# Encoder trunk: memory keys of layer 1 first, residual pieces turned by DMA, first loads in another order

## The chip, the core and the metric

The kernel runs on one core of a Trainium2 chip. The metric is the device time of one execution in microseconds; the number given for a kernel is the median of its timed runs. A profiled execution has a time of its own and a span (from the first to the last instruction in the trace).

## What is computed

Two encoder layers over 256 tokens of width 2048, in float32, each followed by a SwiGLU block. A layer norms x, makes one combined projection for a token mixer and for four memory heads, joins their outputs, projects back and adds. Layer 0 mixes by spatial gating, layer 1 by grouped-query attention with rotary tables. In both, the memory heads attend to 256 memory tokens, whose keys and values come from `mem` alone:

```python
def memory_attention(q_mem, mem, g_mem, w_kv, g_mq, g_mk):
    kv = rms_norm(mem, g_mem) @ w_kv
    k, v = jnp.split(kv, 2, axis=-1)
    k = rms_norm(k.reshape(B, -1, MEM_HEADS, HEAD_DIM), g_mk)
    q = rms_norm(q_mem.reshape(B, S, MEM_HEADS, HEAD_DIM), g_mq)
    s = jnp.einsum('bshd,bmhd->bhsm', q, k).astype(jnp.float32) * (HEAD_DIM ** -0.5)
    p = jax.nn.softmax(s, axis=-1).astype(v.dtype)
    return jnp.einsum('bhsm,bmhd->bshd', p, v)

for l in range(DEPTH):
    h = rms_norm(x, g_mix[l])
    # layer 0: z = h @ w_in_a, gating; layer 1: z = h @ w_in_b, attention; q_mem is the last part of z
    x = x + jnp.concatenate([tok_out, mem_out], axis=-1) @ w_out[l]
    x = x + swiglu(rms_norm(x, g_ffn[l]), w_gate_up[l], w_down[l])
```

## The kernel before

Every float32 operand is split into two parts, a rounded `hi` (ScalarE) and the rest `lo` (VectorE), and each product is made of three matmuls (`matmul3`, L181 to L183). The left operand are the *parts* of an activation, 16 chunks of 128 features by 256 tokens; the right one are weights, loaded raw by SP into buffers of four chunks (`raw`, four of them), cast to `whi` (L265) and subtracted to `wlo` (L266), three buffers of four chunks each.

A `Linear` makes 512 output columns from 16 chunks: 96 matmuls of 512 columns into two of four PSUM banks (`acc`). After every two chunks (12 matmuls) it calls `tick()`, which advances a clock and runs what other code has put off with `later(delay, fn)`; this, and the order of the program, gives the order of the work around the matmuls. The compiler's scheduler then orders each engine's queue by readiness and by that order.

Parts are made in four ways. At the start, x already turned is loaded in eight pieces (`load_turned`) and split by `gained_pair` (`first_piece`, L237 and L238); the squares for its norm come from x itself, loaded by `load_x` and squared by `first_squares` (L207). The memory tokens, also turned already, are loaded on GpSimd's queue and split by the same `gained_pair` (`Memory.prep`: eight loads, each split three ticks after). Between layers, a piece of the new x (512 columns of 128 tokens) is turned either by PE (`norm_piece`: four transposes at L187, into PSUM) or by a DMA transpose (`turned`: a copy that parts the 16-bit halves, L194, the DMA on ScalarE's queue, L195, and a copy that joins them, L200), and then split by `gained` (L225, L226). `residual_turns` takes the DMA for the columns j = 0, 1, which are complete while the last pair of the down projection still runs, and PE for j = 2, 3. Attention heads are turned by PE (`heads_T`, `turn`).

Attention is a chain on later ticks: `head_norm` (squares L449, factors L455, scaling L459, which reads the linear's banks), `queries`, `scores` (exponentials L513, scaling L518), `turn` (transposes L528), `weigh`; four delays say at which ticks.

All parts and attention tiles of a layer's mixer come from one room of 36 tiles (`big`, `MIX_TILES`); a tile that finds none free waits. The room of layer 1 lies on the memory of layer 0's feed-forward room.

Layer 0 runs: warm-up matmuls on an identity, the first linear in pieces of one and two chunks as they land, three linears of v, q_mem, memory keys, memory values, three of u, the output projection. Layer 1 runs:

```python
load_tables(1)
m.prep(20, 2)
acc = linear(hT, w, TOK)                      # own keys
own["v"] = scaled(linear(hT, w, TOK + MEMW), norm.r)
for c in range(3):                            # three groups of queries
    acc = linear(hT, w, c * NB)
    attend(head_norm(acc, norm.r, ghead["q"], True), (5, 6, 10, 13), ...)
m.attend(linear(hT, w, TOK + 2 * MEMW), norm.r, cat)
m.keys()
m.values()
```

The functions that the change touches, with the line numbers of the profile:

Of the kernel before, what the change touches and what calls it, by code (L numbers as in the profile page):

```python
# [17 lines left out]
P = 128  # L18
# [37 lines left out]
def encoder(ctx: ExitStack, tc: tile.TileContext, x, x_t, mem, mem_t, columns, w_in_a, g_v_a, spatial_t, w_in_b,  # L56
# [14 lines left out]
    def nm(s):  # L71
        uid[0] += 1
        return f"{s}_{uid[0]}"
# [195 lines left out]
    class Linear:  # L269
# [3 lines left out]
            self.parts, self.w, self.n0, self.left, self.first, self.raw = parts, w, n0, nk, True, {}  # L273
            self.acc = [psa.tile([P, NB], F32, tag="acc", name=nm("acc")) for _ in range(NT)]

        def fetch(self, k0, n):
            raw = wp.tile([P, KC4, NB], F32, tag="raw", name=nm("raw"), bufs=RAW_TILES)
            src = self.w[k0 * P:(k0 + n) * P, self.n0:self.n0 + NB]
            nc.sync.dma_start(raw[:, :n], src.rearrange("(c p) n -> p c n", p=P))
            self.raw[k0] = raw  # L280

        def run(self, units):
            for k0, n in units:
                if k0 not in self.raw:
                    self.fetch(k0, n)
                raw = self.raw.pop(k0)
                parts = halves(raw[:, :n], n, KC2)
                for s in range(0, n, KC2):
                    m = min(KC2, n - s)
                    self.left -= m  # L290
                    for t in range(NT):
                        for c in range(m):
                            matmul3(self.acc[t], self.parts.get(k0 + s + c, t), parts[s + c],
                                    self.first and c == 0, self.left == 0 and c == m - 1)
                    self.first = False
                    tick()
            return self.acc
# [270 lines left out]
    class Memory:  # L568
# [5 lines left out]
        def prep(self, delay, apart):  # L574
            def load(i):
                m = big(shape=[P, 2, S])
                nc.gpsimd.dma_start(m, mem_t[:, 2 * i:2 * i + 2])
                later(3, lambda: gained_pair(m, i, gslice("mem", self.l), self.parts, big))
                if self.l == 0:
                    j, t = i // 2, i % 2  # L580
                    rows = big()
                    nc.gpsimd.dma_start(rows, mem[0, t * P:(t + 1) * P, j * NB:(j + 1) * NB])
                    later(3, lambda: squares(rows, j, t))

            def squares(rows, j, t):
                self.norm.add(rows, t, j)
                if (j, t) == (3, NT - 1):
                    self.norm.finish(self.r)

            for i in range(8):  # L590
                later(delay + apart * i, lambda i=i: load(i))

        def keys(self):
            acc = linear(self.parts, w_mem_kv[self.l], 0)
# [6 lines left out]
        def values(self):  # L601
            self.V = scaled(linear(self.parts, w_mem_kv[self.l], NB), self.r)

        def attend(self, acc, r, parts):
            attend(head_norm(acc, r, ghead[f"mq{self.l}"]), (4, 13, 17, 19), lambda: self.kT, lambda: self.V, lambda h: h,
                   TOK // P, parts)

    def add_residual(acc, j, norm, g, parts, dma):

# [12 lines left out]
            later(1 + t, lambda t=t: turn(t))  # L622

    def residual_turns(j, norm, g, parts):
        add_residual(None, j, norm, g, parts, j < 2)


    hT = Parts()
# [1 line left out]
    for l in range(DEPTH):  # L630
# [4 lines left out]
        if l == 0:  # L635
# [51 lines left out]

            turned_x = {}
            lin = Linear(hT, w, TOK)
            load_turned(0, nc.scalar)  # L690
            nc.scalar.dma_start(cols, columns)
            nc.scalar.activation(junk[:, :8], mhalf, AF.Square)
            warm_up(9)
            lin.fetch(0, 1)
            lin.fetch(1, 1)
            load_turned(1)
            lin.fetch(2, 2)
            first_piece(0)
            lin.run([(0, 1)])
            load_turned(2)  # L700
            load_turned(3)
            lin.run([(1, 1)])
            first_piece(1)
            lin.run([(2, 2)])
            for i in range(2, 8):
                first_piece(i)
                if i % 2 == 0 and i < 6:
                    load_turned(i + 2)
                    load_turned(i + 3)
                lin.run([(2 * i, KC2)])  # L710
            for t in range(NT):
                for j in range(4):
                    load_x(t, j)
            load_tables(0)
            for j in range(4):
                first_squares(j)
            norm.finish()
            acc = lin.acc
            m.prep(1, 2)
            for i in range(3):  # L720
                later(10 + i, lambda i=i: load_spatial(i))
            for c in range(3):
                if c:
                    acc = linear(hT, w, TOK + c * NB)
                for t in range(NT):
                    v[t][c] = big()
                    nc.scalar.activation(v[t][c], acc[t], AF.Gelu, scale=norm.r[t])
                    square_sum(v[t][c], ssv[t][:, 2 * c:2 * c + 2])
            for t in range(NT):
                gate_rms(t)  # L730
                for c in range(3):
                    later(3 + 3 * t + c, lambda t=t, c=c: gate(t, c))
# [10 lines left out]
        else:  # L743
            w = w_in_b[0]
            own = {}
            load_tables(1)
            m.prep(20, 2)
            acc = linear(hT, w, TOK)
            kn = head_norm(acc, norm.r, ghead["k"], True)

# [5 lines left out]
            for c in range(3):  # L756
                acc = linear(hT, w, c * NB)
                attend(head_norm(acc, norm.r, ghead["q"], True), (5, 6, 10, 13), lambda: own["k"], lambda: own["v"],
                       lambda h, c=c: (4 * c + h) // 3, 4 * c, cat)
            m.attend(linear(hT, w, TOK + 2 * MEMW), norm.r, cat)  # L760
            m.keys()
            m.values()

        hF = Parts()
# [130 lines left out]
```

## Time and profile before

| | |
|---|---|
| timed runs | 2009.22 us median of three, 2007.90 to 2009.52 |
| profiled execution | 2011.89 us, span 2010.0 us |
| mean granted TensorE clock | 0.998 |
| busy: PE, VectorE, ScalarE, GpSimd | 99%, 79%, 60%, 3% |
| first matmul of the first linear | 6.78 us after the span's start |
| first matmul of layer 1 | 1007.5 us |
| first matmul of layer 1's memory keys | 1156.95 us |

In the profile, PE is TensorE's matmuls, PEld its weight loads, DVE VectorE, ACT ScalarE, POOL GpSimd, SP the engine that issues most DMAs. A row of the timeline begins with start and duration in us; in brackets stands how long the engine was idle before and what released it. Matmuls overlap: one of 512 columns is shown with 0.39 us, while a new one starts every 0.23. PEclk is the granted share of TensorE's clock. A group of instructions gives count, busy us and mean ns of one, then idle time before them and its releasers.

### The profile page before, as it was taken

Reading aid. Unit: us, or ns where it says so; the run is one execution under the profiler, and the core shown is the slowest. Engines: PE = TensorE matmul, PEld = TensorE weight load, DVE = VectorE, ACT = ScalarE, POOL = GpSimd, SP = SyncE. Lnnn points to the kernel's source line nnn. Section 1 sums busy time; section 2 is a strip of 40 time slices with the busy share of each in tenths; the row PEclk is TensorE's granted clock in tenths of the full one; section 3 lists DMA queues with packets and bytes.
Section 4 is the critical chain, followed back from the end, with each engine's and each line's share of the span. In section 5 each row is a group of like instructions: output and inputs, shape, how many; then the busy total and the mean of one; then the engine's idle time right before and its main releaser. Section 6 shows DMA issues by size and latency. Waiting matters only on the chain.

```text
span 2010.0 us, 23977 instructions
## 1 busy us (share of the span) xinstructions
PE 1994.3 (99%) x8996; PEld 1652.5 (82%) x8996; DVE 1587.4 (79%) x1686; ACT 1204.0 (60%) x1450; POOL 60.3 (3%) x88
## 2 busy tenths in 40 slices
PE   8999999999999999999999999999999999999999
PEld 7888888888888888887888888888888888888787
DVE  5755558998988989886666876699988889888877
ACT  7755475666446664465765665856764467644662
POOL 2100001000000000000011000010000000000000
PEclk9999999999999999999999999999999999999999
DMA  9854675676666776657766434756766567665674
GB/s 354 288 177 159 194 214 182 206 218 212 220 209 189 213 217 223 208 187 230 224 220 199 163 122 154 217 188 198 229 214 219 189 199 232 214 214 188 199 209 147
DMA packets 266404, 413.85 MB, mean 206 GB/s; under 512 B 74640, under 2 KB 74896, under 8 KB 266288
## 3 DMA queue, kind: packets, MB, share of 16 engines
q1 hardware_dynamic: 199808, 387.62, 58.1%
q10 hardware_dynamic: 63792, 16.19, 4.7%
q0 software_dynamic: 2688, 8.52, 1.3%
q8 instruction: 70, 1.15, 0.2%
q14 instruction: 46, 0.38, 0.1%
HBM read 394.45 MB, written 2.10 MB: 197 GB/s over the span
## 4 chain that ended last, share of the span: by engine, by line
PE 93%; DMA 3%; DVE 2%; ACT 1%; issue 1%; ACTq 0%; SPq 0%; DVEq 0%
PE acc L183 27%; PE acc L182 27%; PE acc L181 27%; PE m L183 4%; PE m L181 4%; PE m L182 4%; DMA a<-a 2%; DVE wlo L266 1%; ACT whi L265 1%; PE m L187 1%; DMA a<-in_x_t 0%; DMA x<-in_x 0%; PE m L528 0%; PE m L661 0%; DMA raw<-in_w_in_a 0%
## 5 line engine op out<-in xcount | busy, mean ns | idle before, releaser
L266 DVE TENSOR_TENSOR wlo<-raw,whi 128x2048 fp32r<-128x2048 f32 (+2 forms) x465 | 841.2, 1824 | 280.4 <-ACT whi L265 267.7
L265 ACT CAST whi<-raw 128x2048 fp32r<-128x2048 f32 (+2 forms) x465 | 705.9, 1538 | 474.8 <-PE acc L182 375.1
L181 PE MATMUL acc<-whi,h 128*128 128x512 f32 x1440 | 561.9, 391 | 4.5 <-ACT whi L265 2.7
L182 PE MATMUL acc<-whi,h 128*128 128x512 f32 x1440 | 561.6, 390 | 0.0
L183 PE MATMUL acc<-wlo,h 128*128 128x512 f32 x1440 | 516.3, 391 | 0.8 <-DVE wlo L266 0.8
L181 PE MATMUL acc<-whi,a 128*128 128x512 f32 x1062 | 414.3, 391 | 1.2 <-DVE a L459 1.2
L182 PE MATMUL acc<-whi,a 128*128 128x512 f32 x1062 | 414.4, 390 | 0.0
L183 PE MATMUL acc<-wlo,a 128*128 128x512 f32 x1062 | 399.1, 390 | 0.2 <-DVE wlo L266 0.2
L181 PEld LDWEIGHTS acc<-whi,h 128*128 128x128 f32 x1440 | 270.6, 188 | 61.1 <-ACT whi L265 4.0
L183 PEld LDWEIGHTS acc<-wlo,h 128*128 128x128 f32 x1440 | 270.8, 188 | 58.6 <-DVE wlo L266 2.9
L182 PEld LDWEIGHTS acc<-whi,h 128*128 128x128 f32 x1440 | 270.9, 188 | 56.2 <-DVE h L238 0.4
L181 PEld LDWEIGHTS acc<-whi,a 128*128 128x128 f32 x1062 | 199.8, 188 | 43.2 <-DVE a L459 1.6
L183 PEld LDWEIGHTS acc<-wlo,a 128*128 128x128 f32 x1062 | 199.8, 188 | 41.7 <-DVE wlo L266 0.6
L182 PEld LDWEIGHTS acc<-whi,a 128*128 128x128 f32 x1062 | 199.7, 188 | 40.9
L265 ACT CAST whi<-T 128x1536 fp32r<-128x1536 f32 x82 | 121.4, 1480 | 103.4 <-PE acc L182 93.8
L266 DVE TENSOR_TENSOR wlo<-T,whi 128x1536 fp32r<-128x1536 f32 x82 | 143.6, 1751 | 11.0 <-ACT whi L265 11.0
L364 DVE TENSOR_TENSOR T<-raw 128x1024 f32<-128x1024 f32 x82 | 100.0, 1220 | 21.5 <-DMA raw<-in_w_gate_up 20.7
L181 PE MATMUL m<-whi,a 128*128 128x512 f32 x264 | 102.8, 390 | 0.2 <-ACT whi L265 0.2
L183 PE MATMUL m<-wlo,a 128*128 128x512 f32 x264 | 102.8, 389 | 0.1
L182 PE MATMUL m<-whi,a 128*128 128x512 f32 x264 | 102.7, 389 | 0.0
L200 ACT COPY sg<-a 128x1024 uint16<-128x1024 uint16 x44 | 51.5, 1169 | 47.0 <-DMA a<-a 46.8
L441 DVE TENSOR_TENSOR e<-acc,e 128x512 f32<-128x512 f32 x88 | 58.1, 684 | 2.5 <-PE acc L183 2.5
(120 smaller groups left out, 1432.9 us busy)
## 6 DMA issues: line engine op xcount, KB each, us to landing
raw<-in_w_gate_up SPq DMA_DIRECT2D x352, 512.0 KB, 4.4
raw<-in_w_down SPq DMA_DIRECT2D x176, 512.0 KB, 4.9
raw<-in_w_out SPq DMA_DIRECT2D x32, 1024.0 KB, 5.3
raw<-in_w_in_a SPq DMA_DIRECT2D x24, 1024.0 KB, 5.3
raw<-in_w_in_b SPq DMA_DIRECT2D x24, 1024.0 KB, 5.2
raw<-in_w_mem_kv SPq DMA_DIRECT2D x16, 1024.0 KB, 5.1
a<-in_mem_t POOLq DMA_DIRECT2D x16, 256.0 KB, 5.3
raw<-in_w_in_a SPq DMA_DIRECT2D x7, 512.0 KB, 7.2
```

The lines of the kernel that those rows point to most:

```text
L181: nc.tensor.matmul(out, lhsT=a[0], rhs=b[0], start=start, stop=False)
L182: nc.tensor.matmul(out, lhsT=a[1], rhs=b[0], start=False, stop=False)
L183: nc.tensor.matmul(out, lhsT=a[0], rhs=b[1], start=False, stop=stop)
L187: nc.tensor.transpose(dst[:, c * P:(c + 1) * P], src[:, c * P:(c + 1) * P], ident)
L200: nc.scalar.copy(halves, back.rearrange("p (h n) -> p n h", h=2))
L265: nc.scalar.copy(hi[:, cut], raw[:, cut])
L266: nc.vector.tensor_tensor(lo[:, cut], raw[:, cut], hi[:, cut].bitcast(F32), ALU.subtract)
L364: nc.vector.tensor_tensor(T[:, :2], raw[:, 1:4:2], w01, ALU.add)
L441: nc.vector.tensor_tensor(o[t][n], self.bank[name], o[t][n], op)
```

## The change

Four edits. The first loads are issued in another order: x_t piece 0 goes on SP, the first linear's weights go whole into four buffers of four chunks (the first in parts of 1, 1 and 2 chunks), sixteen warm-up matmuls stand in place of nine, the squares of x and the Gelu of the first linear are put off to later ticks, and layer 0's memory loads start two ticks later. Layer 1 makes its memory keys first, from parts loaded at once (`prep(-4, 1)`), and makes the same parts a second time (`prep(0, 1)`) for the values, which stay last; the memory chain has shorter delays there. And every residual piece between the layers is turned by DMA.

```diff
-        def fetch(self, k0, n):
-            raw = wp.tile([P, KC4, NB], F32, tag="raw", name=nm("raw"), bufs=RAW_TILES)
-            src = self.w[k0 * P:(k0 + n) * P, self.n0:self.n0 + NB]
-            nc.sync.dma_start(raw[:, :n], src.rearrange("(c p) n -> p c n", p=P))
-            self.raw[k0] = raw
+        def fetch(self, k0, n, cuts=None):
+            if k0 not in self.raw:
+                self.raw[k0] = wp.tile([P, KC4, NB], F32, tag="raw", name=nm("raw"), bufs=RAW_TILES)
+            for c, m in cuts or [(0, n)]:
+                src = self.w[(k0 + c) * P:(k0 + c + m) * P, self.n0:self.n0 + NB]
+                nc.sync.dma_start(self.raw[k0][:, c:c + m], src.rearrange("(c p) n -> p c n", p=P))
...
-        def run(self, units):
+        def run(self, units, step=KC2):
...
-                parts = halves(raw[:, :n], n, KC2)
+                parts = halves(raw[:, :n], n, step)
...
             def load(i):
-                later(3, lambda: gained_pair(m, i, gslice("mem", self.l), self.parts, big))
+                soon(delay + apart * i + 3, lambda: gained_pair(m, i, gslice("mem", self.l), self.parts, big))
...
+            now = clock[0]
+            def soon(at, fn):
+                if now + at <= clock[0]:
+                    fn()
+                else:
+                    later(now + at - clock[0], fn)
             for i in range(8):
-                later(delay + apart * i, lambda i=i: load(i))
+                soon(delay + apart * i, lambda i=i: load(i))
...
-        def attend(self, acc, r, parts):
-            attend(head_norm(acc, r, ghead[f"mq{self.l}"]), (4, 13, 17, 19), lambda: self.kT, lambda: self.V, lambda h: h,
-                   TOK // P, parts)
+        def attend(self, acc, r, parts, waits=(4, 13, 17, 19)):
+            attend(head_norm(acc, r, ghead[f"mq{self.l}"]), waits, lambda: self.kT, lambda: self.V, lambda h: h, TOK // P,
+                   parts)
...
     def residual_turns(j, norm, g, parts):
-        add_residual(None, j, norm, g, parts, j < 2)
+        add_residual(None, j, norm, g, parts, True)
...
-            load_turned(0, nc.scalar)
             nc.scalar.dma_start(cols, columns)
+            load_turned(0)
+            lin.fetch(0, KC4, [(0, 1), (1, 1)])
             nc.scalar.activation(junk[:, :8], mhalf, AF.Square)
-            warm_up(9)
...
+            warm_up(16)
             load_turned(1)
+            lin.fetch(0, KC4, [(2, 2)])
+            for i in (2, 3):
+                load_turned(i)
             first_piece(0)
+            lin.fetch(4, KC4, [(0, 2), (2, 2)])
             first_piece(1)
+            for i in (4, 5):
+                load_turned(i)
+            lin.run([(0, KC4)], 1)
+            lin.fetch(8, KC4, [(0, 2), (2, 2)])
...
+            lin.run([(12, KC4)])
             for j in range(4):
-                first_squares(j)
-            norm.finish()
+                later(1 + j, lambda j=j: first_squares(j))
+            later(5, norm.finish)
             acc = lin.acc
-            m.prep(1, 2)
+            m.prep(3, 2)
...
+            later(6, lambda: gated(0, acc))
+            for c in (1, 2):
+                gated(c, linear(hT, w, TOK + c * NB))
...
             load_tables(1)
-            m.prep(20, 2)
+            m.prep(-4, 1)
+            m.keys()
             acc = linear(hT, w, TOK)
...
-            m.attend(linear(hT, w, TOK + 2 * MEMW), norm.r, cat)
-            m.keys()
+            m.prep(0, 1)
+            m.attend(linear(hT, w, TOK + 2 * MEMW), norm.r, cat, (4, 5, 9, 11))
             m.values()
```

More of the change, by code (lines that the diff above doesn't have):

```diff
@@ L582, in load @@
                     nc.gpsimd.dma_start(rows, mem[0, t * P:(t + 1) * P, j * NB:(j + 1) * NB])
-                    later(3, lambda: squares(rows, j, t))
+                    soon(delay + apart * i + 3, lambda: squares(rows, j, t))
             def squares(rows, j, t):
@@ L689, in encoder @@
             lin = Linear(hT, w, TOK)
-            load_turned(0, nc.scalar)
             nc.scalar.dma_start(cols, columns)
+            load_turned(0)
+            lin.fetch(0, KC4, [(0, 1), (1, 1)])
             nc.scalar.activation(junk[:, :8], mhalf, AF.Square)
-            warm_up(9)
-            lin.fetch(0, 1)
-            lin.fetch(1, 1)
+            warm_up(16)
             load_turned(1)
-            lin.fetch(2, 2)
+            lin.fetch(0, KC4, [(2, 2)])
+            for i in (2, 3):
+                load_turned(i)
             first_piece(0)
[L699 to L702, printed above, removed]
+            lin.fetch(4, KC4, [(0, 2), (2, 2)])
             first_piece(1)
-            lin.run([(2, 2)])
-            for i in range(2, 8):
-                first_piece(i)
[L707 to L710, printed above, removed]
+            for i in (4, 5):
+                load_turned(i)
+            lin.run([(0, KC4)], 1)
+            lin.fetch(8, KC4, [(0, 2), (2, 2)])
+            for i in (6, 7):
+                load_turned(i)
+            for i in (2, 3):
+                first_piece(i)
+            lin.run([(4, KC4)])
+            lin.fetch(12, KC4, [(0, 2), (2, 2)])
+            for i in (4, 5):
+                first_piece(i)
+            lin.run([(8, KC4)])
             for t in range(NT):
@@ L714, in encoder, with gated @@
             load_tables(0)
+            for i in (6, 7):
+                first_piece(i)
+            lin.run([(12, KC4)])
             for j in range(4):
-                first_squares(j)
-            norm.finish()
+                later(1 + j, lambda j=j: first_squares(j))
+            later(5, norm.finish)
             acc = lin.acc
-            m.prep(1, 2)
+            m.prep(3, 2)
             for i in range(3):
                 later(10 + i, lambda i=i: load_spatial(i))
-            for c in range(3):
-                if c:
-                    acc = linear(hT, w, TOK + c * NB)
+            def gated(c, acc):
                 for t in range(NT):
```

## The prediction

> **What bounds the kernel now.** I read the page first: TensorE (PE) is busy for the whole span and holds 93% of the chain that ended last, so only matmul work removed, or time in which PE stands or runs at half clock, can move the end.
>
> ```profile
> span 2010.0 us, 23977 instructions
> PE 1994.3 (99%) x8996; PEld 1652.5 (82%) x8996; DVE 1587.4 (79%) x1686; ACT 1204.0 (60%) x1450; POOL 60.3 (3%) x88
> ...
> PE 93%; DMA 3%; DVE 2%; ACT 1%; issue 1%; ACTq 0%; SPq 0%; DVEq 0%
> ```
>
> Then the waits of PE alone. The list is short, and each row sits in a place that the change touches: the first linear (L237, part of L265) and layer 1's attention (L518, L459).
>
> ```profile
> PE acc L181 <- ACT whi L265: 2.7, 3, 1.7
> PE m L528 <- DVE a L518: 2.1, 2, 1.4
> PE acc L181 <- ACT h L237: 1.8, 1, 1.8
> ...
> PE acc L181 <- DVE a L459: 1.2, 2, 0.6
> ```
>
> Third, a table of stretches (us, busy time of each engine, then PEclk). The clock was halved twice, for 3.4 us each, and each time just after PE had stood; a half-clock stretch loses 3.4 x 0.5 = 1.7 us.
>
> ```profile
> core 0: us, PE busy (x) PEld busy (x) DVE busy (x) ACT busy (x) POOL busy (x), PEclk, DMA share, GB/s
> ...
> 7.60:11.02 3.42, 3.42 (x9) 2.65 (x10) 1.79 (x4) 2.63 (x5) 0.30 (x1) 0.50 1.03 388
> ...
> 1157.90:1161.30 3.40, 3.40 (x10) 2.62 (x9) 3.40 (x9) 2.00 (x9) 1.61 (x2) 0.50 0.27 49
> ...
> 971.70:998.60 26.90, 26.90 (x120) 22.31 (x119) 17.72 (x25) 25.57 (x46) 3.68 (x6) 1.00 0.80 223
> 998.60:1007.50 8.90, 8.90 (x41) 7.34 (x41) 6.30 (x7) 3.58 (x9) 0.00 (x0) 1.00 0.86 248
> 1007.50:1029.30 21.80, 21.80 (x105) 18.13 (x104) 15.08 (x27) 14.88 (x34) 3.10 (x6) 1.00 0.60 197
> ```
>
> The sum is made against the profiled execution, 2011.89 us (span 2010.0). The timed runs have a median of 2009.22, 2.7 lower, and differ among themselves by 1.6. I call a "slot" the twelve 512-column matmuls between two ticks.
>
> **Part 1, the start.**
>
> ```profile
> 1.35 3.61 PE L686 MATMUL m<-ident 128*128 128x128 f32 x18 [1.35 <-POOL ident masks.py:199]
> ...
> 5.70 0.62 ACT L265 CAST whi<-raw 128x512 fp32r<-128x512 f32 x1 [0.37 <-DMA raw<-in_w_in_a]
> 6.23 0.90 ACT L237 ACTIVATE h<-a,cols 128x256 fp32r<-128x256 f32 x2
> ...
> 6.78 0.73 PE L181 MATMUL acc<-whi,h 128*128 128x512 f32 x2 [1.82 <-ACT h L237]
> ```
> ```profile
> L181 PE MATMUL acc<-whi,h 128*128 128x512 f32 x32 | 12.9, 416 | 3.6 <-ACT h L237 1.8 <-ACT whi L265 1.8
> ```
> ```profile
> 15.39 7.13 DMA x<-in_x
> 22.60 0.52 ACT junk L207 x2
> ...
> 26.90 0.94 ACT whi L265
> ...
> 35.56 0.45 PE acc L183 x2
> ```
>
> The group of L181 is for the stretch 4.9 to 33.8 us and holds 32 matmuls; with as many of L182 and L183 these are the 96 of the first linear. They run from 6.78 to 33.8 us: 27.0. At the steady 0.45 / 2 = 0.227 us each (last row), 96 take 21.8. So 5.2 us are lost: 1.7 to the half clock, about 2.2 at 27.9 us (1.7 of it as PE's wait for whi, the rest as matmuls that follow singly), and 1.3 in small waits.
>
> What the edits do. (a) Sixteen warm-up matmuls are 32 instructions instead of 18. The 18 ended at 1.35 + 3.61 = 4.96, the last ones at about 0.11 us apart, so 14 more end near 6.4, when the first data are usable: the empty 1.8 us close and the halved stretch should go. (b) x_t piece 0 is issued first on SP, the weights behind it; one more issue ahead of the weights costs about 0.4 us (two weight issues took 0.8), and the activation of L237 need no longer follow two casts. I take the first matmul at 6.5. (c) The raw weights take 4 whole buffers instead of single chunks that used up all four, so all of SP's 17 first loads can be issued without a wait. (d) The squares of x (0.52 us a pair, 22.60 to 26.90) no longer stand on ScalarE ahead of the last cast; they go to ticks 9 to 12, and the Gelu that needs them to tick 14, two ticks before c=2 wants those banks. That holds while x lands before about 31 us; here x landed at 22.5. What is late next: chunk-wise casts (0.62 each, with 0.45 of L237, against 1.36 us of matmuls per chunk) leave a little slack, so I leave 0.5 us of small waits. The linear takes 22.3 and starts 0.3 earlier: -5.0 us. Bounds: -6 (nothing left) and -3 (first data late, or squares in the way elsewhere). Memory loads start two ticks later; the keys of layer 0 still stand at tick 32 and their last piece at 28: nothing.
>
> On (a) the row shows the clock halved after 1.8 us of waiting. The Trainium skill, "TensorE: Matmul & The Clock Gate", section "What's actually happening", has the clock fall only after an idle window of about 3.4 us; by that rule the wait was too short to cost 1.7, and this term would be -3.3. The measurement decides, and the trace disagrees with the rule here.
>
> **Part 2, the border to layer 1.**
>
> ```profile
> L187 PE MATMUL m<-ident,x x16: 271/272/273, 1008.9 to 1014.6; 128*128 128x128 f32 x16
> ```
> ```profile
> 1014.04 0.87 PE m L187 x8
> ```
> ```profile
> L225 ACT ACTIVATE h<-a,cols 128x128 fp32r<-128x128 f32 x16 | 5.1, 399 | 0.0
> L200 ACT COPY a<-a 128x1024 uint16<-128x1024 uint16 x4 | 4.7, 1167 | 0.2 <-DMA a<-a 0.2
> L194 ACT COPY a<-x 128x1024 uint16<-128x1024 uint16 x4 | 4.2, 1042 | 0.4 <-DVE x L441 0.4
> L207 ACT ACTIVATE junk<-x 128x256 f32<-128x256 f32 x8 | 3.3, 414 | 1.1 <-ACT junk L207 0.9 <-ACT a L200 0.2
> ```
> ```profile
> 994.58 0.79 POOL L154 DMA_DIRECT2D a<-in_rope_c  x1 [670.21 <-DVE h L226]
> ...
> 997.72 0.54 POOL L158 DMA_DIRECT2D a<-in_g_k_b  x1
> ```
> ```profile
> a<-in_mem_t POOLq DMA_DIRECT2D x16, 256.0 KB, 5.3
> ```
>
> Removed: 16 PE transposes at 0.87 / 8 = 0.109: -1.7 us. Added on ScalarE: for four pieces the two copies of L194 and L200 (8.9 us) and the issue of four DMA transposes, and eight memory pieces of 0.9 (the price of L237): 7.2. The 0.9 on VectorE for each piece's low part lies beside it; VectorE had 15 of 21.8 us busy.
>
> The keys linear is 21.8 us of PE. ScalarE was busy 14.9 in that stretch; with 8.9 + 7.2 it would be 31. Some moves ahead: 5.3 us were idle in 998.6 to 1007.5, of which only that after the memory pieces land can be used (five of them now stand on POOL behind the table loads, which end at 998.3, and ahead of the two gains that own keys want 16 ticks later; a load of this kind lands in 5.3 us, so near 1003.6). And the turned pieces are not wanted before ticks 12 to 14 of layer 1, 33 us after its start, where the old order wanted them at ticks 4 to 6. What shares the queue and is wanted at once is the memory pieces (one per slot) and the casts (two units ahead, 10.9 us). The nearest row is 971.7 to 998.6: there four pieces were turned beside casts with ScalarE at 25.6 of 26.9, and PE lost nothing. Upper bound: everything queued in program order and the cast of the third unit behind all of it. From 1004: six memory pieces 5.2, four turned pieces 5.1 + 4.7 + 4.2 + squares 4.2 = 18.2, half a cast 1.0: ready at 1028.4, wanted at 1007.5 + 10.9 = 1018.4: 10 us. Lower bound 0. As the near row shows casts passing turned work, I take 2.5.
>
> **Part 3, attention in layer 1.**
>
> ```profile
> 1134.45 0.36 DVE L455 TENSOR_SCALAR s<-s,s 128x4 f32<-128x4 f32 x2
> ...
> 1155.77 1.12 DVE L459 SCALAR_TENSOR_TENSOR a<-acc,s,a 128x128 f32<-128x128 f32 x4
> ```
> ```profile
> 1153.30 1.03 PE L528 MATMUL m<-ident,a 128*128 128x128 f32 x8
> ...
> 1156.95 0.50 PE L181 MATMUL acc<-whi,a 128*128 128x512 f32 x1 [0.58 <-DVE a L459]
> ```
> ```profile
> 1187.61 1.04 PE L528 MATMUL m<-ident,a 128*128 128x128 f32 x8
> ...
> 1190.55 0.50 PE L181 MATMUL acc<-whi,a 128*128 128x512 f32 x1 [0.58 <-DVE a L459]
> ```
>
> Twice PE turns 12 tiles and then waits for a linear's banks until head_norm has read them (L459): 1153.30 to 1156.95 and 1187.61 to 1190.55, 6.6 us for 24 transposes that take some 2.4 at 0.1: 4.2 lost, with the half clock 5.9. Why is L459 late? Its factors stood at 1134.8 and its output is a tile of the 36-tile room. By the code, from tick 37 the room holds tables 2, own keys 4, own values 4 and all 16 memory parts: 26. Ten are left for a chain that takes 6 (normed queries), 4 (turned), 4 (scores), 8 (turned scores) and 4 kept for each group. With keys first the memory parts are gone after tick 8 and 4 turned keys stay: 14 held in place of 26 while the first groups run, so that they run on time and both waits go: -5.9.
>
> Not free: the parts are made again while q_mem and the values run, at most about 13 tiles beside 22 held (tables, own values and keys, memory keys, two finished groups). By my count the third group's turned scores then slip one or two slots, and the memory chain, now in 4, 5, 9, 11 ticks, has two slots to spare before the output projection reads its parts. From nothing to one old wait with its halved clock (2 + 1.7): I take 1.7. Net -4.2. The eight loads that are made again go on POOL's queue; GpSimd is busy 3% of the span.
>
> **Sum.** -5.0 - 1.7 + 2.5 - 4.2 = -8.4: 2003.5 for an execution like the profiled one. The timed runs are shorter than that one by 2.7, as if they hold fewer halved stretches, so of the two (3.4) I count one as saved: 2009.2 - 6.7 = 2002.5.
>
> **Rivals.**
> - *ScalarE becomes the bound at the border* (ends slower). The 10 us bound in place of 2.5, with a halved stretch behind it: 2002.5 + 7.5 + 1.7 = 2011.7. It decides once the stall at the keys is over 9.2 us. For it: 31 us of work for a 21.8 us linear. Against: the stretch from 971.7.
> - *The attention waits stay*, because the second set of parts is made where tiles are short: 2002.5 + 4.2 = 2006.7. For it: 36 tiles against my count of some 35 to 40 at the peak. Against: the parts are freed two a slot by then.
> - *A slow warm-up.* If all 32 go at the mean of the 18, 3.61 / 18 = 0.20 us, they end at 7.8 and hold the first matmul back 1.3: 2003.8. The same page and section call the window free-running, so the moment may differ from run to run; one profile cannot show that.
> - *The keys' first pieces are not there* at 1007.5, because their tiles come free only with the down projection's last parts: a load of 5.3 us in the open and a halved stretch, 2002.5 + 5.3 + 1.7 = 2009.5, no change. For it: L154 waited until 994.58 for a tile.
>
> **Chances.** Forecast 0.52 (own range 1999 to 2006), ScalarE 0.14, attention waits stay 0.18, slow warm-up 0.08, pieces missing 0.08. A measurement here can tell about 0.2%, 4.0 us. Faster than 2005.2: 0.45 + 0.05 + 0.06 + 0.01 = 0.57; slower than 2013.2: 0.07, nearly all from ScalarE; between: 0.36. The range goes from 1998 (both waits gone, no new ones) to 2010.5, which takes in the three middle rivals.
>
> **What would show it.** Right: PE's first linear of about 22 us from 6.5, no 0.5 in PEclk before 15 us; no L187 on x near 1008; L459 within some 10 us of L455; no wait on L459. Wrong: PE waiting at L181 for whi or for a memory piece in the first 22 us of layer 1 with ScalarE full (border term), L518 or L459 again in PE's waits, now near q_mem, values or the output projection (part 3), or a gap between L686 and L181 (part 1). A new wait in layer 0 on the Gelu of c=0 would be one that I have counted at nothing.

## The result and the profile after

The changed kernel takes 2040.47 us (median of four runs, 2036.82 to 2041.6) beside 2009.37 us for the kernel before on the same chip: a ratio of 1.0151, 95% interval 1.0134 to 1.0169. It is 31 us slower; the forecast was 2002.5. The profiled execution took 2040.88 us, its span is 2039.1.

The page of the changed kernel (busy time by engine; shares of the chain that ended last):

```profile
span 2039.1 us, 24020 instructions
PE 2003.9 (98%) x8994; PEld 1657.7 (81%) x8994; DVE 1594.9 (78%) x1703; ACT 1219.5 (60%) x1475; POOL 62.8 (3%) x96
...
PE 91%; DMA 4%; DVE 2%; ACT 2%; issue 1%; POOL 0%; SPq 0%; ACTq 0%; DVEq 0%; POOLq 0%
```

TensorE is "busy" 9.6 us longer with two matmuls fewer, and the span grew by 29.1. The other 19.5 us are time in which TensorE stood. What it waited for (total us, times, longest):

```profile
PE acc L181 <- ACT a L237: 17.3, 5, 6.9
PE acc L181 <- ACT whi L265: 7.9, 3, 4.3
PE acc L183 <- DVE wlo L266: 1.9, 3, 1.1
...
PE m L181 <- DVE a L176: 1.3, 2, 1.0
```

Against the list of before, the rows of layer 1's attention (L528 on L518, L181 on L459; L529, L519 and L460 in the changed kernel) are gone. In their place stand 17.3 us for L237, the making of memory parts, and 7.9 us for the weights' casts. TensorE's timeline puts every large one into two places (the bracket holds the wait and what ended it):

```profile
1.35 6.66 PE L695 MATMUL m<-ident 128*128 128x128 f32 x32 [1.35 <-POOL ident masks.py:199]
...
12.32 0.50 PE L181 MATMUL acc<-whi,h 128*128 128x512 f32 x1 [1.55 <-ACT whi L265]
17.39 0.68 PE L181 MATMUL acc<-whi,h 128*128 128x512 f32 x1 [2.05 <-ACT whi L265]
39.92 0.79 PE L181 MATMUL acc<-whi,h 128*128 128x512 f32 x1 [4.29 <-ACT whi L265]
...
1018.80 1.22 PE L181 MATMUL acc<-whi,a 128*128 128x512 f32 x2 [4.68 <-ACT a L237]
1025.04 0.73 PE L181 MATMUL acc<-whi,a 128*128 128x512 f32 x2 [0.74 <-ACT a L237]
1032.77 1.22 PE L181 MATMUL acc<-whi,a 128*128 128x512 f32 x2 [4.66 <-ACT a L237]
1045.17 1.22 PE L181 MATMUL acc<-whi,a 128*128 128x512 f32 x2 [6.91 <-ACT a L237]
```

Each long wait costs twice. The table of stretches (same columns as before; PEclk is third from the end) shows the clock at half behind it, and the link full in the start:

```profile
12.30:17.50 5.20, 3.12 (x13) 2.29 (x14) 3.19 (x7) 3.35 (x6) 0.00 (x0) 1.00 1.05 387
17.50:21.00 3.50, 3.50 (x9) 2.73 (x10) 3.37 (x5) 3.30 (x6) 0.00 (x0) 0.51 1.05 385
...
38.00:44.90 6.90, 4.98 (x12) 3.92 (x13) 4.16 (x5) 6.89 (x14) 5.91 (x12) 0.51 0.98 325
...
1018.80:1025.00 6.20, 5.49 (x12) 3.80 (x12) 0.90 (x2) 0.88 (x3) 5.84 (x12) 0.54 0.90 288
```

Lateness below is the start of a matmul in one profiled execution minus that of the same matmul, counted in order, in before's. The second linear starts at 39.92 instead of 33.81 (+6.1), the third 8.5 us late, and this holds through layer 0, whose feed-forward part gave 2.0 back. At the border the lateness goes from 6.5 to 29.3 us, layer 1's attention (up to the second linear of the output projection) brings it to 26.8, and its feed-forward part adds 2.1. So there are two places to explain: the start (+8.5) and the border (+22.8).

**The start, read from the chain of waits** (start, length, what; the link between two rows is what released what):

```profile
3.05 10.33 DMA a<-in_x_t
13.39 8.97 DMA a<-in_x_t
22.38 6.92 DMA x<-in_x
29.39 0.52 ACT junk L207 x2
...
38.25 0.69 ACT a L742
38.93 0.94 ACT whi L265
39.92 0.79 PE acc L181
```

A load of x_t issued at 3.05 took 10.33 us, and the next one in the chain went out only when it had landed. SyncE's own timeline (SPq means an issue by SyncE) shows what followed:

```profile
13.39 1.88 SPq L683 DMA_DIRECT2D a<-in_x_t  x2
16.29 1.73 SPq L281 DMA_DIRECT2D raw<-in_w_in_a  x2
18.32 7.78 SPq L135 DMA_DIRECT2D x<-in_x  x8
26.51 3.96 SPq L281 DMA_DIRECT2D raw<-in_w_in_a  x4
```

The second linear's first weights were issued at 26.51, behind all eight loads of x, and on ScalarE their first cast (38.93) stood behind the squares of x (L207, 29.39 on) and the first Gelu (L742), although the first of these weights had landed at 33.97.

**The border.** GpSimd's timeline, then ScalarE's:

```profile
1005.36 0.54 POOL L578 DMA_DIRECT2D a<-in_mem_t  x1
1016.40 1.23 POOL L165 TENSOR_SCALAR s<-s 128x1 f32<-128x1 f32 x1 [10.50 <-DVE s L256]
...
1021.10 3.85 POOL L578 DMA_DIRECT2D a<-in_mem_t  x7
```
```profile
1018.26 0.89 ACT L237 ACTIVATE a<-a,cols 128x256 fp32r<-128x256 f32 x2
1024.47 0.91 ACT L237 ACTIVATE a<-a,cols 128x256 fp32r<-128x256 f32 x2 [5.32 <-DMA a<-in_mem_t]
...
1030.90 1.16 ACT L200 COPY a<-a 128x1024 uint16<-128x1024 uint16 x1 [2.22 <-DMA a<-a]
...
1032.21 0.91 ACT L237 ACTIVATE a<-a,cols 128x256 fp32r<-128x256 f32 x2
...
1043.30 1.16 ACT L200 COPY a<-a 128x1024 uint16<-128x1024 uint16 x1 [2.65 <-DMA a<-a]
...
1044.61 0.91 ACT L237 ACTIVATE a<-a,cols 128x256 fp32r<-128x256 f32 x2
```

Only one of the eight memory loads went out early. The other seven stood in GpSimd's queue behind a norm operation that waited 10.50 us for VectorE, and left at 1021.10, when the keys linear had begun (1018.80). Yet a late load is what TensorE waited for only once, and for 0.74 us (the second piece, landed at 1024.45). The other three long waits are for pieces that had landed while their parts (L237) stood in ScalarE's queue:

- The first piece landed at 1013.62. ScalarE was busy without a stop from 1013.93 (casts, and squares of the new x), and made its parts at 1018.26; TensorE went on at 1018.80.
- The third and fourth landed at 1025.31 and 1026.90, all eight by 1029.91. Their parts came at 1032.21 and 1044.61, behind copies (L200) that waited 2.22 and 2.65 us for a DMA transpose, and release TensorE at 1032.77 and 1045.17.

### The profile page after: what moved, and what is told of

Its sections match the earlier page's. It is cut to its first block, busy times and chain, and to the rows that moved or that the text cites. A ratio compares the mean times of both kernels' runs of the same rounds, so it can differ in the third digit from the quotient of the medians.

```text
span 2039.1 us, 24020 instructions
## 1 busy us (share of the span) xinstructions
PE 2003.9 (98%) x8994; PEld 1657.7 (81%) x8994; DVE 1594.9 (78%) x1703; ACT 1219.5 (60%) x1475; POOL 62.8 (3%) x96
## 4 chain that ended last, share of the span: by engine, by line
PE 91%; DMA 4%; DVE 2%; ACT 2%; issue 1%; POOL 0%; SPq 0%; ACTq 0%; DVEq 0%; POOLq 0%
PE acc L183 26%; PE acc L182 26%; PE acc L181 26%; PE m L183 4%; PE m L181 4%; PE m L182 4%; DMA a<-a 2%; DVE wlo L266 1%; DMA a<-in_x_t 1%; ACT whi L265 1%; PE m L187 1%; ACT junk L207 0%; PE m L529 0%; DMA x<-in_x 0%; DMA raw<-in_w_gate_up 0%
## 5 line engine op out<-in xcount | busy, mean ns | idle before, releaser
L181 PE MATMUL acc<-whi,h 128*128 128x512 f32 x1440 | 564.0, 392 | 7.9 <-ACT whi L265 7.9
L181 PE MATMUL acc<-whi,a 128*128 128x512 f32 x1062 | 414.6, 393 | 17.3 <-ACT a L237 17.3
L181 PEld LDWEIGHTS acc<-whi,h 128*128 128x128 f32 x1440 | 271.3, 188 | 64.5 <-ACT whi L265 9.2
L181 PEld LDWEIGHTS acc<-whi,a 128*128 128x128 f32 x1062 | 200.4, 189 | 60.8 <-ACT a L237 19.9
L181 PE MATMUL m<-whi,a 128*128 128x512 f32 x264 | 102.8, 389 | 0.0
L200 ACT COPY sg<-a 128x1024 uint16<-128x1024 uint16 x44 | 51.6, 1173 | 39.8 <-DMA a<-a 39.3
L194 ACT COPY a<-sg 128x1024 uint16<-128x1024 uint16 x44 | 45.9, 1042 | 25.1 <-DVE sg L839 10.5
```

Of the source, the lines that this page charges most:

```text
L181: nc.tensor.matmul(out, lhsT=a[0], rhs=b[0], start=start, stop=False)
L194: nc.scalar.copy(planes.rearrange("p (h n) -> p h n", h=2), src.bitcast(U16).rearrange("p (n h) -> p h n", h=2))
L200: nc.scalar.copy(halves, back.rearrange("p (h n) -> p n h", h=2))
```

## The experiments

Absolute times shift by a few microseconds between chips, so each kernel is judged by its ratio to the kernel before on the same chip. "Before" below means that kernel. The gaps of TensorE that the expectations give are 0.3 to 0.4 us longer than the waits in the profile's brackets, which stand in the text.

| kernel | start | border by DMA | layer 1 | ratio | 95% interval | us of 2010 |
|---|---|---|---|---|---|---|
| changed kernel | new | all | keys first | 1.0151 | 1.0134 to 1.0169 | +30 |
| start_only | new | j < 2 | old | 1.0042 | 1.0029 to 1.0056 | +8 |
| dma_only | old | all | old | 1.0014 | 1.0005 to 1.0024 | +3 |
| keys_only | old | j < 2 | keys first | 1.0032 | 1.0019 to 1.0045 | +6 |
| no_start | old | all | keys first | 1.0105 | 1.0088 to 1.0122 | +21 |
| keys_sp | old | j < 2 | keys first, loads on SyncE | 1.0018 | 1.0007 to 1.0030 | +4 |
| dma_three | old | j < 3 | old | 1.0019 | 1.0009 to 1.0029 | +4 |
| dma_pool | old | all, copied back by GpSimd | old | 0.9997 | 0.9987 to 1.0006 | -1 |
| keys_third | old | j < 2 | keys third | 0.9995 | 0.9983 to 1.0007 | -1 |
| start_weights | new, next weights ahead of x | j < 2 | old | 0.9993 | 0.9984 to 1.0002 | -1 |
| start_gate | the same, later loads held | j < 2 | old | 1.0018 | 1.0009 to 1.0027 | +4 |
| start_gate2 | the same, x held too | j < 2 | old | 1.0007 | 0.9996 to 1.0018 | +1 |
| gate_third | start_gate's | j < 2 | keys third | 1.0012 | 1.0002 to 1.0022 | +2 |
| gate2_third | start_gate2's | j < 2 | keys third | 0.9997 | 0.9988 to 1.0006 | -1 |
| sum_two | start_weights' | j < 2 | keys third | 0.9999 | 0.9990 to 1.0008 | 0 |
| sum_three | start_weights' | all, by GpSimd | keys third | 1.0001 | 0.9991 to 1.0011 | 0 |

### One part at a time

start_only is before with the change's edits of the start alone, dma_only with `j < 2` set to `True`, keys_only with the edits of layer 1, no_start the change without the edits of the start.

> The new first loads, warm-up and put-off squares alone, layer 1 and the border as before. Theory A (the parts add up, and the start lost what its own stretch shows: layer 0's second linear began 8.5 us later): 2009.4 + 8.5 = about 2018, with the empty stretch ahead of c=1's first matmul near 35 to 40 us again. Rival (the loss at the start came from something later that pulled on the queues): about 2009.

> All residual pieces between the layers by DMA, everything else as before. Theory A (at the border the memory keys' loads and splits are late; turned pieces alone have no early reader but j = 2, 3 at ticks 4 to 6 of layer 1): -1.7 us for the 16 transposes and a few us of waiting for the late turned pieces, 2008 to 2014. Rival B (ScalarE is the bound at the border, whoever reads first): a stall of 8 us or more, above 2017.

> Layer 1's memory keys first with their parts made twice, residual pieces j = 2, 3 still turned by TensorE. Theory A (the seven later memory loads stand on GpSimd's queue behind the norm's small operations, and the linear reads one piece per slot): one long wait of some 5 us at the second piece stays, the waits behind the DMA transposes go, attention gains about 5: 2009 to 2016. Rival B (only the turned pieces on ScalarE make the stall): no wait for L237, about 2004.

> The whole change but with the old start. Theory A: 2040.5 - 8.5 = about 2032, with the four waits for memory pieces in the first 40 us of layer 1 as in the changed kernel. Rival (the border's loss needs the shifted queues that the new start leaves): under 2020.

Measured: +8, +3, +6, and +21 for the last two together; each time is near theory A's. Start and border are independent (+8 and +21 make the change's +30 within the intervals). start_only has the empty stretch again:

```profile
39.90 0.79 PE L181 MATMUL acc<-whi,h 128*128 128x512 f32 x1 [5.96 <-ACT whi L265]
```

The DMA turn and the early keys are not independent: 3 + 6 = 9, together 21, so about 12 us (7 to 17 by the intervals) come only when both are there. By the traces, at the border alone, it is 6.4 and 8.7 us, together 23.5, so about 8; the rest arises later, where dma_only gets some of its loss back. The readings of 1032.21 and 1044.61 above show where: memory parts that could be made stand behind copies that wait for a transpose. No run has the keys first and the copies off ScalarE, which would test this alone.

In keys_only theory A's time came, but not its mechanism. The seven late loads are there as in the change (they left at 1015.25). But the one long wait is for the first piece, which was loaded early (it landed at 1006.89). Its parts stood on ScalarE behind the casts, the squares and all parts of the last residual pieces (L225), with ScalarE busy without a stop from 1007.65:

```profile
998.69 0.54 POOL L578 DMA_DIRECT2D a<-in_mem_t  x1
```
```profile
1013.05 2.71 ACT L225 ACTIVATE h<-m,cols 128x128 fp32r<-128x128 f32 x10
1015.66 0.90 ACT L237 ACTIVATE a<-a,cols 128x256 fp32r<-128x256 f32 x2
```
```profile
1016.21 1.22 PE L181 MATMUL acc<-whi,a 128*128 128x512 f32 x2 [6.62 <-ACT a L237]
```

After it 6.8 us at half clock follow; the attention behind gives 2.4 us back (lateness 8.9 at the border, 6.5 at the output projection). In dma_only there are no early parts, but casts and residual parts stand behind the same copies. ScalarE, then TensorE:

```profile
1016.54 1.17 ACT L200 COPY a<-a 128x1024 uint16<-128x1024 uint16 x1 [3.67 <-DMA a<-a]
...
1020.37 1.98 ACT L265 CAST whi<-raw 128x1024 fp32r<-128x1024 f32 x2
```
```profile
1019.64 0.50 PE L181 MATMUL acc<-whi,h 128*128 128x512 f32 x1 [1.82 <-ACT h L225]
1025.76 0.80 PE L181 MATMUL acc<-whi,h 128*128 128x512 f32 x1 [2.89 <-ACT whi L265]
```

### What holds the memory loads, and what the DMA turn costs

keys_sp:

```diff
-                nc.gpsimd.dma_start(m, mem_t[:, 2 * i:2 * i + 2])
+                (nc.sync if self.l else nc.gpsimd).dma_start(m, mem_t[:, 2 * i:2 * i + 2])
```

> The kernel before with the memory keys first in layer 1 (the order of keys_only) and old start and border residual, but layer 1's eight memory loads are issued by SyncE instead of GpSimd. In keys_only only the first memory load was issued before layer 0's down projection ended; the other seven stood on GpSimd behind a norm operation that waited 10.89 us for VectorE. Theory A (GpSimd's order holds the loads): on SyncE they are issued several microseconds earlier than in keys_only (the last at 1015.25 there), the 6.9 us gap of TensorE at 1016 shrinks to under 2 us, and the kernel comes to about 2011 to 2014 us beside 2018.7 for keys_only. Theory B (the loads lack room: their tiles lie where layer 0's feed-forward data still stand): they are issued no earlier, the gap stays between 5 and 8 us, the weights behind them on SyncE come late as well, and the time is 2017 to 2022 us.

dma_three:

```diff
-        add_residual(None, j, norm, g, parts, j < 2)
+        add_residual(None, j, norm, g, parts, j < 3)
```

> The kernel before with the third residual column (j = 2) turned by DMA as well, the fourth (j = 3) still by TensorE: half of dma_only's edit. Theory A (the end of the border is what costs: the last column's DMA turn starts only when the last linear's evictions are done, and ScalarE's copies wait for it): j = 3 alone carries the loss, so this kernel is within 1.5 us of before or up to 1 us faster (8 transposes less, twice). Theory B (each column turned by DMA costs its part of ScalarE and queue time): half of dma_only's loss, 1.5 to 2 us slower than before.

dma_pool (dma_only, and the copy L200 of the border on GpSimd):

```diff
-            nc.scalar.copy(halves, back.rearrange("p (h n) -> p n h", h=2))
+            back_copy(halves, back.rearrange("p (h n) -> p n h", h=2))
```

> dma_only (all sixteen pieces... that is, all eight border tiles turned by DMA, everything else as before) with one thing changed: the copies back from a DMA transpose at the border (L200 of dma_only) run on GpSimd instead of ScalarE, so that no ScalarE cast stands behind a wait for a DMA transpose. Theory A (ScalarE's order is the loss: a copy that waits 3.67 us for its DMA holds the casts of the next weights): TensorE's gaps of 2.2 and 3.3 us at 1020 and 1026 go and the kernel comes to 1 us under to 0.5 us over the kernel before. Theory B (the turn itself is too slow, from sum to parts: the parts come too late whoever copies them): the gaps stay or grow with GpSimd's slower copies, and the kernel is 3 to 6 us slower than before.

keys_sp came between its two theories. SyncE issued the loads again in two lots, the second behind weight loads and 1.5 us earlier than in keys_only, but the first one 10 us later:

```profile
1008.71 0.45 SPq L578 DMA_DIRECT2D a<-in_mem_t  x1
...
1013.76 3.58 SPq L578 DMA_DIRECT2D a<-in_mem_t  x7
```

That one landed at 1014.19, its parts were begun at 1014.21, ahead of most of L225's work this time, and TensorE went on at 1014.77. Its wait halved (3.2 for 6.6 us), its half-clock time did not, and the ratio went from 1.0032 to 1.0018 with intervals that overlap, so that keys_sp is better is not shown. The wait is for the load here and for ScalarE's order in keys_only. Among SyncE's waits the loads of L578 themselves have 0.6 us in all; they wait their turn behind others. So queue order holds them, and not, at the time of issue, a missing tile. Why the compiler's scheduler orders them so late on either queue (it may expect no free tile) is not settled.

dma_three has one more column turned by DMA than before, and its ratio is no smaller than that of two more (1.0019 and 1.0014). Both its theories expected less. Its ScalarE shows a copy L200 at 1018.15 that waited 3.32 us: that one such copy in front of the casts is enough is argued from this, not shown.

dma_pool takes just this wait off ScalarE, and the loss is gone (0.9997, theory A). GpSimd now does the waiting, with nobody behind it in a hurry:

```profile
1017.64 1.99 POOL L200 COPY a<-a 128x1024 uint16<-128x1024 uint16 x1 [5.62 <-DMA a<-a]
```

One TensorE wait of 1.7 us is left at the border and no half clock. That a waiting copy in ScalarE's queue was the cost of the DMA turn is thereby shown for dma_only, with one open end: the scheduler moved more than the copy. In both kernels three copies L194 stand ahead of the next casts, which come at 1016.32 for 1020.37, but four of the parts (L225) went from ahead of them to behind them.

### Keys third

keys_third is before with (in layer 1) the parts loaded one tick apart from the first tick, the keys behind own keys and own values, and the values last:

```diff
-            m.prep(20, 2)
+            m.prep(1, 1)
...
             own["v"] = scaled(linear(hT, w, TOK + MEMW), norm.r)
+            m.keys()
...
-            m.attend(linear(hT, w, TOK + 2 * MEMW), norm.r, cat)
-            m.keys()
+            m.prep(0, 1)
+            m.attend(linear(hT, w, TOK + 2 * MEMW), norm.r, cat, (4, 5, 9, 11))
```

> The kernel before with its start and border residuals as they are (columns 2 and 3 by TensorE). In layer 1 the memory parts are made at the own-key linear (loads from the first tick, one unit apart), the memory keys come third, behind own keys and own values, the memory values stay last with parts made a second time during the q-groups' last units, and the attention to memory uses shorter waits (4, 5, 9, 11). Theory A (the loss of keys_only is the border alone: loads and parts that come too late for a first linear): nothing stands at the border, so its loss of 9 us goes to under 2 us, the gain of 4.5 us in the attention phase stays, and the kernel ends 1 to 5 us faster than before, 2004.5 to 2008.5 us. Theory B (the parts cost ScalarE wherever they are made early): a loss of 4 us or more shows in own keys and own values instead, and the time is 2010 to 2016 us.

Measured 0.9995. Nothing is lost at the border (5.6 us late before it and behind it; the 5.6 came in layer 0, where the kernels are alike), and the attention brings it to 3.1: 2.4 us gained, as in the change. Theory A holds for the border; the gain lies below the 4.5 us that it named, and too low for the timed runs to show. Here four memory loads went out in a row (2.13 us from 1003.68) where the change and keys_only had one, and two linears stand ahead of the reader.

### The start

start_weights (start_only with one edit):

```diff
             lin.run([(8, KC4)])
+            after = Linear(hT, w, TOK + NB)
+            after.fetch(0, KC4)
+            after.fetch(4, KC4)
             for t in range(NT):
                 for j in range(4):
                     load_x(t, j)
```

> start_only with one thing changed: the next linear's first two weight loads (c = 1 of layer 0's first input matrix) are issued on SyncE ahead of the eight loads of x, and ScalarE so casts its first unit before the squares of x and the Gelu. Theory A (the start's loss is mainly the order at the end of the first linear): TensorE's gap of 6.35 us at 39.9 shrinks to under 1.5 us, and half or more of start_only's loss goes: 2012 to 2015.5 us beside 2020.3. Theory B (the first loads' crowding, 1.9 to 2.4 us gaps at 12 and 17, is the main part): the gap at 39.9 only moves to another place and the time stays above 2017 us.

Measured 0.9993 for start_only's 1.0042: theory A; by the ratio the whole loss is gone. The edit moves the weights on SyncE, and with them their casts on ScalarE; the two are not told apart. TensorE's wait of 5.96 us at 39.9 in start_only is now 0.49; the one at 12 is left:

```profile
12.11 0.79 PE L181 MATMUL acc<-whi,h 128*128 128x512 f32 x1 [2.39 <-ACT whi L265]
...
39.97 0.51 PE L181 MATMUL acc<-whi,h 128*128 128x512 f32 x1 [0.49 <-ACT whi L265]
```

start_gate issues the later x_t loads and the weights by turns and holds x_t back (a GpSimd write of eight columns into the load's tile, made from a finished part); start_gate2 sets that hold earlier and holds the loads of x as well:

```diff
+            def hold(some, after):
+                seen = hT.get(2 * after + 1, 0)[1][:, :8].bitcast(F32)
+                nc.gpsimd.tensor_scalar(some, seen, 1.0, 0.0, ALU.mult, ALU.add)
```

> start_weights with the first loads held back: SyncE waits with the third and later loads of x_t (and the weights behind them) until the first parts are made, by a small GpSimd write into the tile of the third load, and in the same way before the fifth and the seventh. Theory A (loads in flight share the bandwidth, about 387 GB/s from 10 to 30 us, so loads issued early for later use delay the one needed next): the second half of the first weights lands about 2 us earlier, TensorE's gap of 2.78 us at 12.1 and the half clock behind it go, and the kernel comes 2 to 4 us under start_weights, 1.5 to 4.5 us under the kernel before. Theory B (the gap comes from SyncE's issue order and the latency of a load, not from sharing): the waits only move the gap, and the time is within 1 us of start_weights or above it.

> start_gate with the hold on the later x_t loads set earlier (all on the second piece's parts) and the eight loads of x held as well, until the sixth piece's parts are made. In start_gate the hold worked where it was set (no gap at 12, TensorE at full clock until 21.5 us), but the loads of x, which nothing held, went out from 9.75 us in front of the held x_t loads and TensorE stood 5.08 us at 23.8. Theory A (the order in which bytes are served decides, since the link is full at about 387 GB/s): with x behind the first linear's data, the gap at 23.8 goes, the second linear starts 2 to 5 us earlier than in the kernel before (33.8), and the kernel is 1.5 to 5 us under before. Theory B (the first linear is bound by the link's total, 6 MB for its inputs, whatever the order): TensorE stops elsewhere in the first 34 us and the time is within 1.5 us of before or above it.

> start_gate's start and keys_third's layer 1 together, the border as in the kernel before. If the two places are independent, the time is the sum of both: keys_third took about 1 us off the kernel before (2.5 us in the attention phase of its trace, some of it lost to late weights elsewhere), start_gate is expected to take off 1.5 to 4.5 us, so 2.5 to 6 us under the kernel before. If one shifts the other's transfers, less than the larger of the two is left.

> start_gate2's start with keys_third's layer 1 (memory keys behind own keys and own values, values last), border as before. Independent places: the gain of start_gate2 plus about 1 to 2.5 us, so 2.5 to 7 us under the kernel before; were the two dependent, less than the larger of the two.

The hold did what it should at 12 us: in start_gate no wait of 2.39 us and no half clock there, so loads that come in too early do delay the one that is needed (in one trace, with the order of issue changed as well). But the bytes that passed in front became the next wait. SyncE, then TensorE, in start_gate:

```profile
9.75 2.35 SPq L135 DMA_DIRECT2D x<-in_x  x3
...
19.90 3.10 SPq L686 DMA_DIRECT2D a<-in_x_t  x2
```
```profile
23.81 0.79 PE L181 MATMUL acc<-whi,h 128*128 128x512 f32 x1 [4.69 <-ACT whi L265]
```

With x held too, TensorE ran almost without a stop until 19 us, and then waited once more, for x_t parts (L237) that stood on ScalarE behind two casts, which waited for their weights. ScalarE, then TensorE, in start_gate2:

```profile
18.35 1.05 ACT L265 CAST whi<-raw 128x1024 fp32r<-128x1024 f32 x1 [2.96 <-DMA raw<-in_w_in_a]
20.81 1.04 ACT L265 CAST whi<-raw 128x1024 fp32r<-128x1024 f32 x1 [1.41 <-DMA raw<-in_w_in_a]
21.76 3.30 ACT L237 ACTIVATE h<-a,cols 128x256 fp32r<-128x256 f32 x8
```
```profile
22.32 0.73 PE L181 MATMUL acc<-whi,h 128*128 128x512 f32 x2 [2.95 <-ACT h L237]
```

start_gate2 is at 1.0007, theory B's figure by the clock; by its trace the order still decides where TensorE stops. From 2 to 22 us the link moved about 7.1 MB there (297, 372, 365, 362 and 388 GB/s in five stretches of 4 us), while the first linear needs 6.3 MB (4.2 of weights, 2.1 of x_t). So the total alone does not force the stop at 22, and a better order may exist; none was found. gate_third and gate2_third, which add keys_third's layer 1, came at +2 and -1: the sum of two gains that was expected had nothing to add up, since neither start was a gain. The Trainium skill, "DMA: Bandwidth & Descriptors", section "Specifications", gives about 358 GB/s as the limit of one core, half of what two share. Here one core ran, and several stretches of 4 us moved 385 to 395, so the limit of this start is higher than that share.

### Parts together

> start_weights' start and keys_third's layer 1 together, border as in the kernel before. Theory A (the parts are independent): the two ratios 0.9993 and 0.9995 multiply to 0.9988, about 2.4 us under the kernel before. Theory B (both were noise, or one gives back what the other takes): within 1 us of the kernel before.

> sum_two with the border's eight tiles turned by DMA and copied back by GpSimd, as in dma_pool. Theory A: independent, 0.9988 times 0.9997, about 3 us under the kernel before. Theory B: in keys_third's order GpSimd issues layer 1's memory loads at the border and ScalarE makes their parts at once; the copies stand in the same GpSimd queue, so loads or copies come late as in the changed kernel, and it is 2 to 8 us slower than sum_two, with TensorE waiting for memory parts (L237) or residual parts (L225) between 1015 and 1050 us.

Both are within 0.1% of before. For sum_two that is theory B's figure; sum_three came as neither of its theories. In sum_three's trace the DMA turn and early memory parts stand beside each other with 0.4 us of waiting for L237, so the interaction is gone once no ScalarE copy waits for a transpose and the keys are not the first linear; which of the two is needed was not tried. No version made here is faster than before by more than the measurement can tell.

## Why the prediction was wrong

**Part 1 (-5.0, came +8.5).** Three of its four steps failed.

- Step (a): the half clock after the warm-up did go, in all nine traces with 32 instructions. But here these ran at 0.21 us (6.66 / 32) and held the first matmul to 7.8: the rival "slow warm-up" came true with its 1.3. That is luck of the execution: in start_gate the same 32 took 5.31 us and the first matmul came at 6.41, because the full clock was granted at 4.46 there and at 7.30 here.
- Step (c), "all of SP's 17 first loads can be issued without a wait": they could not. SyncE issued one more only as one issued eight loads earlier had landed, and most of the weights took 9 to 11 us to land where before they took 7.2. The link was as full in before (393 and 388 GB/s from 10 to 18 us), so it is not the rate that changed but which bytes went first. I counted issue slots and not bytes: loads put early share the link with the one that TensorE needs. This is the wait at 12.32 and 17.39. start_gate shows the sharing by taking one of them away.
- Step (d) looked at the squares against the last cast of the first linear and the Gelu's own deadline. Its condition held but for 0.3 us: the last load of x landed at 31.3 (in before at 24.6; the 22.5 that I took was that of one of the eight). What I left out is who stands behind them: the next linear's first cast on ScalarE and its first weights on SyncE. start_weights shows that this is most of the loss.

**Part 2 (+0.8 net, came +22.8).** The saving of the transposes is real: dma_only gains 1.7 us on before between 1007.5 and 1014.7, where before has them. The term of 2.5 for ScalarE was the one mis-sized: with the saving taken off, it came as 24.5. Its method failed: I added up ScalarE's work and took 971.7 to 998.6, where casts flowed past turned work, as the nearest row. In that stretch the copies L200 had waited 0.2 us for their transposes in all; at the border they waited 2.22 and 2.65 us, with parts and casts behind them.

The rival of a full ScalarE was right for the first wait alone (busy without a stop from 1013.93 to 1019.15). At the later ones it is not full (9.35 us busy in the 12.4 from 1032.8); it waits in order, and the rival's 10 us for one stall were too few. The sentence that five memory loads would stand on GpSimd ahead of the gains failed: one did, and it landed at 1013.62, not near 1003.6. The rival "the keys' first pieces are not there" named the effect; its cause (tiles that come free late) is not borne out, and its 7.0 held for one wait, where four came. I also summed edits that meet in one queue: about 8 of the 22.8 us are their interaction.

**Part 3 (-4.2, came -2.4).** The waits on L459 and the half clock behind one are gone, with L528's rows. The saving was too large by 0.9: the waits of the list, 2.1 and 1.2, and a halved stretch of 1.7 make 5.0, where I had read 5.9 off the timeline. The new waits are 1.6 (1.3 for L176, 0.3 for L237), about the 1.7 that I allowed; some 1.0 us more is not located. Why the waits went is less sure than I wrote. The scaling of the second and third group of queries and of q_mem began 12.9, 21.3 and 27.2 us after its factors before and 6.0, 12.3 and 17.1 in the changed kernel: shorter, as a freer room would have it, but not within the 10 us of my sign, and no run changes the number of tiles alone.

**Profiled and timed runs.** I took one halved stretch off for the timed runs; here the two differ by 0.4 us and nothing hangs on it.

## What to carry to other kernels

Before work is put on an in-order queue, ask not only how full the engine is but which of its instructions wait, for how long, and who stands behind them: in dma_only a copy that waited 3.67 us came with a loss of about 3 us, and with the same copies on GpSimd there was none. Loads issued early are not free when the link is full; the order of bytes is the schedule, and the first load of the next stage belongs ahead of data whose use is later. Edits that share a queue should be priced together.

## What the runs showed of the hardware

In each of the 17 traces the moments at which the granted clock changes lie a whole number of steps of 3.41 us apart. In the changed kernel it is at half from 17.54 to 20.95, 38.02 to 44.84, 1017.64 to 1024.47, 1031.30 to 1038.12 and 1041.54 to 1048.36. While there was work left, it fell at the end of a step in which TensorE had stood for 1.8 us or more in all, and stayed where that was 1.7 or less, about half a step (one step with 1.64 fell, one with 1.74 stayed). It came back at the end of the first step with at most 0.6 us of standing; steps with 0.8 or more stayed at half, which is why it lasts 3.41 us after a short wait and 6.83 after most long ones.

So the same wait can cost nothing or 1.7 us by where it falls. In before, 1.82 us (4.97 to 6.78) lie inside one step and the clock fell at its end, 7.60. In dma_only the 1.82 before 1019.64 are cut by the end of a step at 1018.15, and it did not fall; nor did it for 1.93 in start_only (before 16.98, cut at 16.65) and 2.12 in start_gate2 (before 1875.29, cut at 1874.23). And waits add up: before's second halving, at 1157.90, follows 1.26 and 0.58 us within one step.

The Trainium skill, "TensorE: Matmul & The Clock Gate", section "What's actually happening", has the clock fall after an idle window of about 3.4 us in a count that runs freely. The traces agree with the length and with the free count; they do not agree that a whole window must be idle, since 1.8 us of one was enough here.
